# A transformer layer on one Trainium2 core: eight modulation units of the second norm's scale become whole rows summed by VectorE

## The chip, the cores and the metric

One core of a Trainium2 chip runs the whole layer in one launch. The metric is the device time of that launch in microseconds (us), as the median of several executions. The engines are TensorE (PE in the profile, its weight loads PEld), VectorE (DVE), ScalarE (ACT), GpSimd (POOL) and SyncE (SP), which issues nearly all DMAs here from one queue, in order. PE, ACT and DVE take their instructions in the order in which the program hands them over.

## The reference

One layer of a diffusion backbone on 128 context tokens and 512 latent tokens, width 1024, float32. Every norm is followed by a scale and a shift, and every branch by a gate; these six vectors are products of a conditioning vector with slices of `w_ada`, one vector for the context tokens and one for the latent ones:

```python
sh1, sc1, g1, sh2, sc2, g2 = jnp.split(ada, N_ADA, axis=-1)   # ada = silu(c) @ w_ada + b_ada, (.., 6 * 1024)
u = rms_norm(h, p["g_pre1"]) * (1 + sc1) + sh1
mo, k, v = mixer(u, p, rope_tabs, ctx_k, ctx_v)               # attention @ w_att_out, conv @ w_conv_out, gates, @ w_o
h = h + g1 * rms_norm(mo, p["g_post1"])
u = rms_norm(h, p["g_pre2"]) * (1 + sc2) + sh2
h = h + g2 * rms_norm(conv_ffn(u, p), p["g_post2"])
```

The change is about how `sc2`, the second norm's scale, is computed: 2 x 1024 numbers from 4 MB of weights. It is needed only when the second norm's output is turned and scaled, in the second half of the product with `w_o`.

## The kernel before

**Products in two parts.** Each float32 operand is cut into a rounded high part (ACT, `hi_of` L1253 or `split` L199) and a remainder (DVE, `lo_of` L1257 or `split` L200), and each product is made of three matmuls, high by high, high by low and low by high (`mm3`, L234 to L236, or `block`, L1266). So for each 512 KB of weights that SP loads into a `raw` slot (three of them), ACT and DVE each make one part (`whi`, `wlo`) before PE can use it.

**The stages that matter here**, in order of time:

- *Attention's output projection* (loop `for j in range(KT)`, 8 visits). Each visit cuts the next weights, makes some sums of the matrix that the next stage multiplies (`making`), and runs `plain_gemm`: 48 matmuls of 320 columns into two PSUM banks, `(2n + h) % 8` for visit n. Behind visits 0 to 4 stands `ada2_mm`: two *modulation units*, each 128 columns of `w_ada` (all 1024 rows, loaded by `ada2_load`, L283), multiplied by the conditioning vectors on PE in 32-column strips of its array (L289). Units 0 to 7 are the scale, units 8 and 9 the first quarter of the shift. DVE adds each pair's result to `acc` (L1485, L1487), and after visit 5 one small matmul and three DVE instructions (`ada2_fold`) put all ten into `mod`. Pair j is summed in bank `(2 * j + 4) % 8`, but pair 0 in bank 2.
- *The mixer's input products* (19 products, `mix`). Here the rest of the shift is already made from whole rows: SP loads 128 rows of `w_ada` at a time, DVE multiplies them by the conditioning value of its partition and sums them (`gate_add`, L341 for the first rows, L343 for the others), once for each of the two conditioning vectors, and at the end PE sums over the partitions with four matmuls against ones (`gate_sums`, L352).
- *w_conv_out* (8 visits of `plain_gemm`). Each visit on DVE: the next weights' low part, two multiplies by the gate (L1451), one addition (L1626), the low part of the result (L1280). Between them stand two `gate_add` of 1024 columns, which make the first gate, `g1`, from whole rows in the regions `GA0` and `GA1` (5 rows each).
- *The first half of w_o* (`for q in range(4)`, quarters of 30 matmuls of 512 columns: 5 token tiles, two blocks of 128 rows). Between the quarters PE sums the gate (`gate_sums`), DVE finishes it (`gate_rows`, L356 and L357), and SP writes it out and reads it back spread over all partitions. Loads and cuts for the second half run beside it (`half_load`, L2013; `half_cut`), and rooms are opened in `GA0` and `GA1` for the next product's right sides (`more_right`, which gives `ZBr`).
- *The second half of w_o*, in which each token tile is normed, scaled and shifted as it comes (`turn2`, L1735; `modulated`, L1746, which reads `mod`).

**What sets the order.** PE, ACT and DVE run in the order written out; SP's too up to the end of w_conv_out (`loads`), and from there a scheduler places SP's DMAs.

Of the kernel before, what the change touches and what calls it, by code (L numbers as in the profile page):

```python
# [20 lines left out]
KT = 8  # L21
# [90 lines left out]
def trunk_layer(ctx, tc, x_prompt, x_sample, cache_k, cache_v, c, c_ctx, w_ada, b_ada, g_pre1, g_post1, g_pre2,  # L112
# [30 lines left out]
    def nm(s):  # L143
        cnt[0] += 1
        return f"{s}_{cnt[0]}"
# [149 lines left out]
    def ada2_load(i, room=None):  # L295
        ada_raw[i] = raw_tile() if room is None else room
        ada_load(ada_raw[i], (4, 3)[i // KT] * D + (i % KT) * 128)

    def ada2_mm(us, p=None):

        p = (ps1() if p is None else p)[:, 0:128]
        for i in us:
            ada_mm(p, ada_raw[i], 2 * (i % 16), i == us[0], i == us[-1])
        return p
# [6 lines left out]
        else:  # L311
            V.tensor_tensor(out=a, in0=a, in1=p, op=ALU.add)

    def ada2_fold(acc, p=None):
        p = ps1() if p is None else p
        PE.matmul(p[:, 0:32], acc[:, 0:128], sel, start=True, stop=True)
        for which, nf in ((0, KT), (1, KT // 4)):
            src = p[:, 16 * which:16 * which + 2 * nf].rearrange("p (f r) -> p r f", r=2)
            b = F_B + (4, 3)[which] * KT
            V.tensor_tensor(out=mod[:, which, :, 0:nf], in0=src, in1=feat[:, b:b + nf].unsqueeze(1).broadcast_to((128, 2, nf)), op=ALU.add)  # L320
            if which == 0:
                V.tensor_tensor(out=mod[:, which], in0=mod[:, which], in1=feat[:, F_PRE2:F_PRE2 + KT].unsqueeze(1).broadcast_to((128, 2, KT)),
                                op=ALU.mult)


    def gate_load(raw, kind, k, c0=0):
        nc.sync.dma_start(raw, w_ada[k * 128:(k + 1) * 128, kind * D + c0:(kind + 1) * D])
# [974 lines left out]
    ada_rooms = {}  # L1302

    def ada2_fetch(i):
        h = i // 2 % 2
        if i % 2 == 0:
            ada_rooms[h] = rb.tile([128, 2, 1024], F32, tag=("r6b", "r5b")[h], name=nm("ada"))
        ada2_load(i, ada_rooms[h][:, i % 2])

    def quad(x, i):  # L1310
        return x[:, i * 4 * HT:(i + 1) * 4 * HT].rearrange("p (k c) -> p k c", k=4)
# [142 lines left out]


    acc = WB[:, 3200:3328]
    for i in range(4):
        ada2_fetch(i)
    for j in range(KT):
        unit = next_unit()  # L1460
        if j == 6:
            for n in range(3):
                mload(n)
        if j < 6:
            for f in making[2 * j:2 * j + 2]:
                f()
        elif j == 7:
            adds = msums(0)
            adds[0]()
            mhi(0, 0)  # L1470
            lo_of(("m", 0, 0))
            adds[1]()
            mhi(0, 1)
            adds[2]()
            mload(3)
        outs = plain_gemm(j, *unit.parts, AH, AL)
        for out, (b0, b1) in zip(outs, BLKS):
            if j < 2:
                times(MA[:, j, b0:b1], out, MA[:, KT - 2 + j, b0:b1])
            else:  # L1480
                S.activation(MA[:, j, b0:b1], out, AF.Copy)
        if j < 5:
            p = ada2_mm((2 * j, 2 * j + 1), bank((2 * j + 4) % 8 if j else 2))
            if j == 0:
                V.tensor_copy(acc, p)  # L1485
            else:
                V.tensor_tensor(out=acc, in0=acc, in1=p, op=ALU.add)  # L1487
            if j < 3:
                for i in (2 * j + 4, 2 * j + 5):
                    ada2_fetch(i)  # L1490
        elif j == 5:
            ada2_fold(acc, bank((2 * j + 4) % 8))


    BH = Halves(NTOK, F32R, "BH")
# [100 lines left out]

    GA0, GA1 = (region(ra, f"r{i}", [5, D], F32, f"GA{i}") for i in range(2))
    gaccs, gvec = [[GA0[:, i, :]] for i in range(2)], GA0[:, 4, :].rearrange("p (i c) -> p i c", i=2)
    graws = [GA1[:, k, :] for k in range(5)] + [GA0[:, k, :] for k in (2, 3)] + [GA1[:, 0, :]]


    loads = ctx.enter_context(ExitStack())
# [1 line left out]
    for j in range(KT):  # L1604
        if j + 1 < KT:
            vcut(j + 1)
        else:
            cut_upto(state["next"] + 1)
        if 0 < j < KT - 3:
            mload(2 * NP + j + 3)  # L1610
        elif j:
            fetch(state["next"] + min(j - 4, 2))
        if j == 0:
            gate_load(graws[0], 2, 0)
        if j < KT - 1:
            gate_load(graws[j + 1], 2, j + 1)
        if j == 5:
            gate_vectors(gvec, 2, g_post1)
        _, hi, lo = cut["v", j]
        outs = plain_gemm(j + 2, hi, lo, BH, BL)  # L1620
        sg = ROWS[j]
        for h, (out, (b0, b1)) in enumerate(zip(outs, BLKS)):
            times(sg[:, b0:b1], out, sg[:, b0:b1])
            if h == 0 and j:
                gate_add(gaccs, graws[j], j, 0)
        V.tensor_tensor(out=sg, in0=sg, in1=MA[:, j, :], op=ALU.add)  # L1626
        for row in range(0 if j == 0 else 1, 2):
            gate_add(gaccs, graws[j], j, row)
        mh, ml = MH[j // 4][:, j % 4, :], ML[j // 4][:, j % 4, :]
        S.activation(mh, sg, AF.Copy)  # L1630
        minus(ml, sg, mh.bitcast(F32))
# [12 lines left out]
        z = ra.tile([128, 2, 4, HALF], F32R, tag=f"r2{x}", name=f"ZB{i}")  # L1644
        TT[i] = (z[:, 0], z[:, 1])

    def more_right():
        for names, tag in ((("B11", "B21"), "r0"), (("B22", "T2"), "r1")):
            z = ra.tile([128, 4, 4, HALF], F32R, tag=tag, name=f"ZB{tag}")
            for a, i in enumerate(names):  # L1650
                TT[i] = (z[:, 2 * a], z[:, 2 * a + 1])

    QUAD = {f"{i + 1}{j + 1}": UFS[i][:, :, j * HALF:(j + 1) * HALF] for i in range(2) for j in range(2)}

# [365 lines left out]
    us = []  # L2020
    for q in range(4):
        us.append(next_unit())
        if q == 0:
            half_load(3)
            taps_load()
            for t in range(3):
                row_load(t)
            half_cut(3, lent("T3"))
        elif q == 1:
            half_load(0)  # L2030
            p = bank(6)
            gate_sums(p, gaccs)
            gate_rows(p, gvec, GA0[:, 3, 0:512], 0)
            half_cut(0)
        elif q == 2:
            half_load(1)
            plain_load(0, 0)
            plain_load(0, 1)
            for row in (1, 0):
                bload(WR[:, row, :], 0, row)  # L2040
            ffn_taps(bank(7))
        else:
            more_right()
            half_cut(1)
            half_load(2)
            for i, name in ((0, "T2"), (1, "T1")):
                hi_of((0, i), raws[0, i], lent(name))
                lo_of((0, i))
                plain_load(1, i)
        for t in range(NT):  # L2050
            if q == 0:
                PA[t] = bank(t)
            for k in (2 * q, 2 * q + 1):
                sl = slice(t * 128, (t + 1) * 128)
                mm3(PA[t], MH[k // 4][:, k % 4, sl], ML[k // 4][:, k % 4, sl], *us[q].at(k % 2), k == 0, k == KT - 1)


    KORDER = (0, 1, 2, 3, 6, 7, 4, 5)
# [307 lines left out]
```

## Time and profile before

| | us |
|---|---|
| three executions | 1092.72, 1093.31, 1094.11 (median 1093.31) |
| the profiled execution | 1094.45 |
| its span, first to last instruction | 1092.6 |
| DVE busy | 852.3 (78%) |
| ACT busy | 584.8 (54%) |
| DMA, mean over the span | 139 GB/s |

A row of a timeline reads: start, duration, engine, line of the program, operation, output and inputs, count, and in brackets how long the engine had been idle and what ended that. Matmuls overlap, so a row's duration is longer than its share of PE's time; starts of neighbours tell what a step costs. `SPq` is a DMA's issue on SP's queue. Names are the program's, without buffer numbers: `b` is a PSUM bank, `MHa` to `MLb` the two parts of w_o's left side, `GA` the two regions of row sums, `ada` the modulation units' weights, `s` the conditioning vectors.

### The profile page before, as it was taken

What the parts mean: (1) busy time and instruction counts of PE and PEld (TensorE: products, weight loads), DVE (VectorE), ACT (ScalarE), POOL (GpSimd) and SP (SyncE); (2) the same over time, 40 slices, a digit from 0 to 9 for tenths busy, and PEclk for the clock granted to TensorE, in tenths of its full rate; (3) what the DMA queues carried; (4) which work ended last, traced back from release to release, by engine and by line L of the source; (5) the groups of instructions that cost most, each with busy time, mean ns of one, the idle gap of its engine ahead of it and who ended that gap; (6) DMA issues with size and microseconds to landing.
All of it is one profiled execution on the core that took longest, in us unless ns stands there. A gap on an engine that the chain in (4) does not pass through costs nothing.

```text
span 1092.6 us, 20419 instructions
## 1 busy us (share of the span) xinstructions
PE 1073.0 (98%) x8155; PEld 998.1 (91%) x8155; DVE 852.3 (78%) x1313; ACT 584.8 (54%) x1050; POOL 130.9 (12%) x163
## 2 busy tenths in 40 slices
PE   8999999999999999999999999999999999999997
PEld 6788888899999999999999789999999999998886
DVE  5687888855578999987488368889999988989544
ACT  5468989952345454545423366655546555545442
POOL 1077666600000000000000020000000000000001
PEclk9999999999999999999999999999999999999999
DMA  9828999997144333332445634324434433335722
GB/s 322 246 69 159 168 163 189 180 179 204 58 119 126 95 92 93 91 95 86 152 135 184 195 128 136 103 91 125 137 106 131 137 102 110 120 102 197 271 78 97
DMA packets 245613, 152.18 MB, mean 139 GB/s; under 512 B 94602, under 2 KB 224134, under 8 KB 245518
## 3 DMA queue, kind: packets, MB, share of 16 engines
q1 hardware_dynamic: 245406, 150.84, 51.1%
q8 instruction: 64, 1.05, 0.4%
q14 instruction: 31, 0.25, 0.1%
q10 hardware_dynamic: 112, 0.04, 0.0%
HBM read 117.39 MB, written 11.44 MB: 118 GB/s over the span
## 4 chain that ended last, share of the span: by engine, by line
PE 87%; DVE 5%; DMA 4%; ACT 2%; issue 1%; POOL 0%; DVEq 0%; SPq 0%; ACTq 0%
PE b L1266 44%; PE b L234 10%; PE b L236 10%; PE b L235 10%; PE s L689 5%; PE s L1065 2%; PE s L1162 1%; DMA PT<-P 1%; DVE marks L1112 1%; DMA araw<-in_w_ada_dram 1%; PE s L234 1%; DMA raw<-in_w_in_dram 1%; DVE wlo L1257 1%; PE s L236 1%; PE s L235 1%
## 5 line engine op out<-in xcount | busy, mean ns | idle before, releaser
L1266 PE MATMUL b<-ZBr,whi 128*128 128x320 f32 x688 | 152.2, 309 | 0.0
L1266 PE MATMUL b<-MT,whi 128*128 128x320 f32 x608 | 134.3, 309 | 0.3 <-DVE WA L1277 0.3
L1266 PEld LDWEIGHTS b<-ZBr,whi 128*128 128x128 f32 x688 | 115.0, 188 | 0.1
L1266 PE MATMUL b<-ZBr,wlo 128*128 128x320 f32 x344 | 106.3, 309 | 0.0
L1266 PEld LDWEIGHTS b<-MT,whi 128*128 128x128 f32 x608 | 101.6, 188 | 0.6 <-issue 0.6
L1266 PE MATMUL b<-MT,wlo 128*128 128x320 f32 x304 | 94.1, 309 | 0.0
L1253 ACT ACTIVATE whi<-SUM 128x1024 fp32r<-128x1024 f32 x40 | 42.2, 1056 | 78.7 <-DVE SUM L1800 76.1
L1830 DVE SCALAR_TENSOR_TENSOR Y<-C,cffn,Y 128x642 f32<-128x642 f32 x88 | 77.6, 882 | 0.9
L1266 PE MATMUL b<-ZBT,whi 128*128 128x320 f32 x320 | 71.0, 309 | 0.0
L1266 PE MATMUL b<-UL,whi 128*128 128x320 f32 x228 | 70.8, 311 | 0.0
L1253 ACT ACTIVATE whi<-WB 128x1024 fp32r<-128x1024 f32 x38 | 40.1, 1055 | 56.4 <-DVE WB L1367 56.4
L1266 PE MATMUL b<-UH,wlo 128*128 128x320 f32 x228 | 70.1, 307 | 0.0
L1266 PE MATMUL b<-UH,whi 128*128 128x320 f32 x228 | 69.7, 306 | 0.0
L1257 DVE TENSOR_TENSOR wlo<-raw,whi 128x1024 fp32r<-128x1024 f32 (+1 forms) x51 | 50.4, 1018 | 22.6 <-ACT whi L1253 22.6
L200 DVE TENSOR_TENSOR wlo<-raw,whi 128x1024 fp32r<-128x1024 f32 (+1 forms) x31 | 34.2, 1102 | 40.3 <-ACT whi L199 39.8
L1266 PEld LDWEIGHTS b<-ZBr,wlo 128*128 128x128 f32 x344 | 64.6, 188 | 0.3 <-DVE wlo L1257 0.3
L1274 ACT ACTIVATE p<-b 128x320 f32<-128x320 f32 x78 | 34.2, 438 | 55.1 <-PE b L1266 53.4
L1266 PEld LDWEIGHTS b<-MT,wlo 128*128 128x128 f32 x304 | 57.0, 188 | 0.3 <-DVE wlo L1257 0.2
L1112 DVE TENSOR_REDUCE marks<-s 128x1 f32<-128x640 f32 x64 | 51.9, 815 | 6.5 <-PE s L1065 6.5
L1266 PEld LDWEIGHTS b<-ZBT,whi 128*128 128x128 f32 x320 | 54.2, 188 | 1.5
L1253 ACT ACTIVATE whi<-raw 128x1024 fp32r<-128x1024 f32 (+1 forms) x51 | 43.5, 892 | 18.4 <-PE b L236 10.0
L1257 DVE TENSOR_TENSOR wlo<-WB,whi 128x1024 fp32r<-128x1024 f32 x38 | 46.5, 1223 | 8.7 <-ACT whi L1253 8.6
(420 smaller groups left out, 3210.5 us busy)
## 6 DMA issues: line engine op xcount, KB each, us to landing
raw<-in_w_in_dram SPq DMA_DIRECT2D x48, 512.0 KB
RAW<-in_w_up_dram SPq DMA_DIRECT2D x40, 512.0 KB
raw<-in_w_down_dram SPq DMA_DIRECT2D x22, 512.0 KB
actd<-Y SPq DMA_DIRECT2D x18, 321.0 KB
ada<-in_w_ada_dram SPq DMA_DIRECT2D x10, 512.0 KB
XT<-in_w_ada_dram SPq DMA_DIRECT2D x9, 512.0 KB
raw<-in_w_att_out_dram SPq DMA_DIRECT2D x8, 512.0 KB
raw<-in_w_conv_out_dram SPq DMA_DIRECT2D x8, 512.0 KB
```

The source lines that it names most:

```text
L200: V.tensor_tensor(out=lo[:, :n], in0=raw, in1=hi[:, :n].bitcast(F32), op=ALU.subtract)
L234: PE.matmul(out, ah, bh, start=start, stop=False)
L235: PE.matmul(out, ah, bl, start=False, stop=False)
L236: PE.matmul(out, al, bh, start=False, stop=stop)
L689: PE.matmul(out, a, b, start=start and n == 0, stop=stop and n == 2, skip_group_check=True)
L1065: PE.matmul(o[h], q_of(hl, i, rows), kk[kx][rows, g, ks], start=m == 0, stop=m == 2, tile_position=(64 * h, 0), skip_group_check=True)
L1112: V.tensor_reduce(out=mk[:, h:h + 1], in_=s_of(), axis=AX.X, op=ALU.max, negate=True)
L1253: S.activation(to[0], raw, AF.Copy)
L1257: V.tensor_tensor(out=lo, in0=raw, in1=hi.bitcast(F32), op=ALU.subtract)
L1266: PE.matmul(out, p[:, ws], q[:, k, :], start=start and k == 0 and n == 0, stop=stop and k == 3 and n == 2, skip_group_check=True)
L1274: S.activation(t, pair[j][b], AF.Copy)
L1830: V.scalar_tensor_tensor(out=y, in0=crows(j)[i][:, d:d + NACT], scalar=cffn[:, 44 * d + o:44 * d + o + 1], in1=y, op0=ALU.mult, op1=ALU.add)
```

## The change

The eight scale units leave the attention projection; its one remaining pair (the two shift units) comes behind visit 1, in bank 6, and is folded behind visit 2 (`shift_fold`). The scale is made from whole rows instead, like the gate: `scale_load` loads 128 rows of `w_ada` (512 KB) into one of three rows of `GA1`, `scale_add` multiplies and adds 1024 columns on DVE, sixteen times in all (eight blocks of rows, two conditioning vectors), into `GA0`. Seven of them stand in w_conv_out's visits 1 to 7, three, two and four in w_o's quarters 0, 1 and 2. Within quarter 3, after its third token tile, PE sums over the partitions (`gate_sums` into bank 7), ACT copies the sums, and behind the quarter PE turns them into columns with four transposes and DVE adds the bias and multiplies by the gain (`scale_columns`, four instructions of 8 columns). The gate's own rows shrink from seven places to two, its finished rows go to `GA1`, and the room in `GA0` is opened only behind the transposes.

```diff
-    def ada2_fold(acc, p=None):
-        p = ps1() if p is None else p
+    def shift_fold(acc, p):
         PE.matmul(p[:, 0:32], acc[:, 0:128], sel, start=True, stop=True)
...
@@ attention's output projection
     acc = WB[:, 3200:3328]
-    for i in range(4):
-        ada2_fetch(i)
+    lent_ada = rb.tile([128, 2, 1024], F32, tag="r6b", name="ada")
+    for i in range(2):
+        ada2_load(KT + i, lent_ada[:, i])
     for j in range(KT):
...
-        if j < 5:
-            p = ada2_mm((2 * j, 2 * j + 1), bank((2 * j + 4) % 8 if j else 2))
-            if j == 0:
-                V.tensor_copy(acc, p)
-            else:
-                V.tensor_tensor(out=acc, in0=acc, in1=p, op=ALU.add)
-            if j < 3:
-                for i in (2 * j + 4, 2 * j + 5):
-                    ada2_fetch(i)
-        elif j == 5:
-            ada2_fold(acc, bank((2 * j + 4) % 8))
+        if j == 1:
+            V.tensor_copy(acc, ada2_mm((KT, KT + 1), bank((2 * j + 4) % 8)))
+        elif j == 2:
+            shift_fold(acc, bank((2 * j + 4) % 8))
...
-    graws = [GA1[:, k, :] for k in range(5)] + [GA0[:, k, :] for k in (2, 3)] + [GA1[:, 0, :]]
+    graws = [GA1[:, k % 2, :] for k in range(KT)]
+    saccs, sraws = [[GA0[:, 2 + i, :]] for i in range(2)], [GA1[:, 2 + k % 3, :] for k in range(KT)]
+
+    def scale_load(k):
+        gate_load(sraws[k], 4, k)
+
+    def scale_add(i):
+        gate_add(saccs, sraws[i // 2], i // 2, i % 2)
+
+    def scale_columns(p, rows):
+        for c in range(4):
+            PE.transpose(p[:, c * 128:(c + 1) * 128], rows[:, c * 128:(c + 1) * 128], ident)
+        to, b = mod[:, 0].rearrange("p r (h c) -> p r h c", h=2), F_B + 4 * KT
+        for f, op, x in ((b, ALU.add, p.rearrange("p (c h r x) -> p r h c x", h=2, r=2, x=32)[:, :, :, :, 0]), (F_PRE2, ALU.mult, to)):
+            for row in range(2):
+                V.tensor_tensor(out=to[:, row], in0=x[:, row], in1=feat[:, f:f + KT].rearrange("p (h c) -> p h c", h=2), op=op)
...
@@ w_conv_out, visit j
         if j < KT - 1:
             gate_load(graws[j + 1], 2, j + 1)
+        for k in ((0,), (1,), (), (2,), (), (3,), (4,), (5,))[j]:
+            scale_load(k)
...
         for row in range(0 if j == 0 else 1, 2):
             gate_add(gaccs, graws[j], j, row)
+        if j:
+            scale_add(j - 1)
...
@@ the first half of w_o
     for q in range(4):
         us.append(next_unit())
+        for i in ((7, 8, 9), (10, 11), (12, 13, 14, 15), ())[q]:
+            scale_add(i)
+            if i in (7, 9):
+                scale_load(i // 2 + 3)
...
             gate_sums(p, gaccs)
-            gate_rows(p, gvec, GA0[:, 3, 0:512], 0)
+            gate_rows(p, gvec, GA1[:, 0, 0:512], 0)
...
-            more_right()
+            more_right(("B22", "T2"), "r1")
...
                 mm3(PA[t], MH[k // 4][:, k % 4, sl], ML[k // 4][:, k % 4, sl], *us[q].at(k % 2), k == 0, k == KT - 1)
+            if q == 3 and t == 2:
+                p = bank(7)
+                gate_sums(p, saccs)
+                S.activation(GA0[:, 0, 0:512], p, AF.Copy)
+    scale_columns(bank(6), GA0[:, 0, 0:512])
+    more_right(("B11", "B21"), "r0")
```

How instructions stand on an engine before and after, at two places. First DVE in w_o's quarters 0 to 2, before, from the low part of quarter 1's weights (the first row) to the convolution taps' copy; `wlo` are weights' low parts, `ZBT` that of the second half's last block, `GA` the gate's two finishing instructions:

```order
L200 TENSOR_TENSOR wlo_7364<-raw_7232,whi_7363 128x1024
L1257 TENSOR_TENSOR ZBT_7359<-raw_7367,ZBT_7359 128x1024
L200 TENSOR_TENSOR wlo_7414<-raw_7361,whi_7413 128x1024
L356 TENSOR_TENSOR GA_6837<-b_537_7419,GA_6837 128x512
L357 SCALAR_TENSOR_TENSOR GA_6837<-GA_6837 128x512
L1257 TENSOR_TENSOR wlo_7431<-raw_7417,whi_7430 128x1024
L200 TENSOR_TENSOR wlo_7465<-raw_7411,whi_7464 128x1024
L1687 COPY cffn<-b_545_7476 128x132
```

And after, the same stretch:

```order
L200 TENSOR_TENSOR wlo_7291<-raw_7155,whi_7290 128x1024
L338 SCALAR_TENSOR_TENSOR GA_6751<-GA_6752,s_81,GA_6751 128x1024 x3
L1252 TENSOR_TENSOR ZBT_7286<-raw_7299,ZBT_7286 128x1024
L200 TENSOR_TENSOR wlo_7346<-raw_7288,whi_7345 128x1024
L338 SCALAR_TENSOR_TENSOR GA_6751<-GA_6752,s_81,GA_6751 128x1024 x2
L351 TENSOR_TENSOR GA_6752<-b_528_7353,GA_6751 128x512
L352 SCALAR_TENSOR_TENSOR GA_6752<-GA_6752,GA_6751 128x512
L1252 TENSOR_TENSOR wlo_7365<-raw_7351,whi_7364 128x1024
L200 TENSOR_TENSOR wlo_7399<-raw_7343,whi_7398 128x1024
L338 SCALAR_TENSOR_TENSOR GA_6751<-GA_6752,s_81,GA_6751 128x1024 x4
L1687 COPY cffn<-b_536_7414 128x132
```

Nine row sums have come in, in groups of three, two and four, each group between the low parts of two weights.

Second SP's queue in the same quarters, before: w_o's weights for quarter 2, then a block of the second half, the residual's rows (`WR`), the taps (`UFb`), the weights for quarter 3, two more blocks of the second half, and the gate's way out (`bct`):

```order
L216 DMA raw_7361<-in_w_o_dram 128x2x512
L2013 DMA raw_7367<-in_w_o_dram 128x2x512
L1682 DMA WR<-in_x_prompt_dram 128x1024
L1682 DMA WR<-in_x_sample_dram 128x1024 x2
L1679 DMA UFb<-in_conv_ffn_dram 88x128
L1679 DMA UFb<-in_conv_ffn_dram 44x128
L216 DMA raw_7411<-in_w_o_dram 128x2x512
L2013 DMA raw_7417<-in_w_o_dram 128x2x512
L2013 DMA raw_7468<-in_w_o_dram 128x2x512
L361 DMA bct<-GA_6837 1x512 x4
```

And after:

```order
L216 DMA raw_7288<-in_w_o_dram 128x2x512
L322 DMA GA_6752<-in_w_ada_dram 128x1024
L1682 DMA WR<-in_x_prompt_dram 128x1024
L1682 DMA WR<-in_x_sample_dram 128x1024
L2013 DMA raw_7299<-in_w_o_dram 128x2x512
L1682 DMA WR<-in_x_sample_dram 128x1024
L1679 DMA UFb<-in_conv_ffn_dram 88x128
L1679 DMA UFb<-in_conv_ffn_dram 44x128
L216 DMA raw_7343<-in_w_o_dram 128x2x512
L322 DMA GA_6752<-in_w_ada_dram 128x1024 x2
L2013 DMA raw_7351<-in_w_o_dram 128x2x512
L2013 DMA raw_7406<-in_w_o_dram 128x2x512
```

Three loads of scale rows (`GA` from `w_ada`) have come in, one ahead of the residual's rows and two ahead of the blocks `raw_7351` and `raw_7406`, which are the second half's blocks 0 and 1.

More of the change, by code (lines that the diff above doesn't have):

```diff
@@ L312, in ada2_keep @@
             V.tensor_tensor(out=a, in0=a, in1=p, op=ALU.add)
-    def ada2_fold(acc, p=None):
-        p = ps1() if p is None else p
+    def shift_fold(acc, p):
         PE.matmul(p[:, 0:32], acc[:, 0:128], sel, start=True, stop=True)
[L317 to L323, printed above, removed]
+        nf = KT // 4
+        V.tensor_tensor(out=mod[:, 1, :, 0:nf], in0=p[:, 16:16 + 2 * nf].rearrange("p (f r) -> p r f", r=2),
+                        in1=feat[:, F_B + 3 * KT:F_B + 3 * KT + nf].unsqueeze(1).broadcast_to((128, 2, nf)), op=ALU.add)
     def gate_load(raw, kind, k, c0=0):
@@ L1301, in trunk_layer @@
     TAG = {"T1": "r5a", "T2": "r5b", "T3": "r6a", "T4": "r6b"}
[L1302 to L1308, printed above, removed]
     def quad(x, i):
@@ L1645, in trunk_layer, with more_right @@
         TT[i] = (z[:, 0], z[:, 1])
[L1647 to L1651, printed above, removed]
+    def more_right(names, tag):
+        z = ra.tile([128, 4, 4, HALF], F32R, tag=tag, name=f"ZB{tag}")
+        for a, i in enumerate(names):
+            TT[i] = (z[:, 2 * a], z[:, 2 * a + 1])
     QUAD = {f"{i + 1}{j + 1}": UFS[i][:, :, j * HALF:(j + 1) * HALF] for i in range(2) for j in range(2)}
```

## The prediction

> **What bounds the kernel now.** I read the page first, then the table of stages (windows of engine time), then the waits of TensorE (PE) in these stages, then the timelines around the edits.
>
> ```profile
> span 1092.6 us, 20419 instructions
> PE 1073.0 (98%) x8155; PEld 998.1 (91%) x8155; DVE 852.3 (78%) x1313; ACT 584.8 (54%) x1050; POOL 130.9 (12%) x163
> PEclk9999999999999999999999999999999999999999
> PE 87%; DVE 5%; DMA 4%; ACT 2%; issue 1%; POOL 0%; DVEq 0%; SPq 0%; ACTq 0%
> ```
>
> PE is busy nearly all the span, at its full clock, and makes 87% of the chain that ends last. The stages of the edits (columns: window and its length, then busy us and instructions of PE, PEld, VectorE (DVE), ScalarE (ACT), POOL; granted clock, DMA share, GB/s), and PE's only wait in the first of them:
>
> ```profile
> 239.30:302.40 63.10, 62.58 (x546) 60.56 (x546) 33.99 (x37) 19.04 (x26) 0.00 (x0) 1.00 0.56 148
> 537.70:594.20 56.50, 56.50 (x386) 56.50 (x385) 43.59 (x52) 14.47 (x18) 0.00 (x0) 1.00 0.53 170
> 594.20:624.40 30.20, 30.20 (x135) 23.36 (x134) 14.40 (x16) 9.22 (x10) 0.00 (x0) 1.00 0.67 217
> PE b L234 <- DVE WB L1485: 0.5, 1, 0.5
> ```
>
> The rows are attention's output projection, w_conv_out, and the first half of w_o. All three are PE's: what leaves PE's queue is gained whole, what enters it is paid whole, and what DVE gets is free until an operand comes late.
>
> **What leaves PE.** Visits 0, 2, 3 and 4 of attention's output projection lose their pair of modulation units; visit 1 keeps one. PE's timeline at visits 0 and 1:
>
> ```profile
> 246.37 0.30 PE L236 MATMUL b<-AHb,wlo 128*128 128x320 f32 x1
> 246.61 1.08 PE L289 MATMUL b<-ada,s 128*32 128x128 f32 x32
> 248.19 0.39 PE L234 MATMUL b<-AHa,whi 128*128 128x320 f32 x1 [0.51 <-DVE WB L1485]
> 248.42 0.31 PE L235 MATMUL b<-AL,whi 128*128 128x320 f32 x1
> ...
> 255.17 0.31 PE L236 MATMUL b<-AHb,wlo 128*128 128x320 f32 x1
> 255.41 1.08 PE L289 MATMUL b<-ada,s 128*32 128x128 f32 x32
> 256.42 0.42 PE L234 MATMUL b<-AHa,whi 128*128 128x320 f32 x1
> 256.67 0.31 PE L235 MATMUL b<-AL,whi 128*128 128x320 f32 x1
> ```
>
> From a visit's second matmul (248.42) to its 48th (255.17) are 46 steps, 0.147 us each. Without the pair the next visit's second matmul would start two steps after 255.17, at 255.46; it starts at 256.67. A pair costs 1.20 us of the path, more than its busy 1.08, since the matmul behind it also starts slowly. After visit 0 it is 248.42 - (246.37 + 0.29) = 1.76: pair 0 writes bank 2, which is visit 1's first output bank, so PE waits 0.51 for DVE to copy the sum out (L1485). The change puts its one pair in bank 6 at visit 1, which visit 3 uses first, so that wait leaves too. The fold (one small matmul) only moves from visit 5 to visit 2. Gain: 1.76 + 3 x 1.20 = 5.36 us. If the wait stayed it would be 4.85. A visit becomes 48 x 0.147 = 7.05 us instead of 8.26. By the stage's row DVE and ACT then have 34 and 19 us of work in some 58, and the changed program drops eight 512 KB loads there, so no other engine binds.
>
> **What enters PE.** In w_o's last quarter come four column sums of 512 and, behind the quarters, four transposes. Both have twins in the trace:
>
> ```profile
> 600.74 0.40 PE L235 MATMUL b<-wlo,MHa 128*128 128x512 f32 x1
> 600.98 0.40 PE L236 MATMUL b<-whi,MLa 128*128 128x512 f32 x1
> 601.30 1.07 PE L352 MATMUL b<-GA,ones 128*32 128x512 f32 x8
> 602.30 0.50 PE L234 MATMUL b<-whi,MHa 128*128 128x512 f32 x1
> 602.63 0.40 PE L235 MATMUL b<-wlo,MHa 128*128 128x512 f32 x1
> ...
> 636.10 0.39 PE L236 MATMUL b<-whi,MLa 128*128 128x512 f32 x1
> 636.33 0.60 PE L1735 MATMUL b<-ident,TX 128*128 128x128 f32 x4
> 636.68 0.48 PE L234 MATMUL b<-whi,MHa 128*128 128x512 f32 x1
> 637.00 0.39 PE L235 MATMUL b<-wlo,MHa 128*128 128x512 f32 x1
> ```
>
> A step is 0.23 to 0.24 (600.74 to 600.98). By the same reckoning the sums cost 602.63 - (600.98 + 0.46) = 1.19 and four transposes 637.00 - (636.10 + 0.46) = 0.44: together 1.63 us, if nothing waits.
>
> **What DVE gets in w_conv_out.** One visit there:
>
> ```profile
> 566.20 0.49 DVE L1451 TENSOR_TENSOR WA<-b,WA 128x320 f32<-128x320 f32 x1 [1.05 <-PE b L236]
> 566.72 0.82 DVE L1626 TENSOR_TENSOR WA<-WA,MA 128x640 f32<-128x640 f32 x1
> 567.47 1.28 DVE L343 SCALAR_TENSOR_TENSOR GA<-GA,s,GA 128x1024 f32<-128x1024 f32 x1
> 568.66 0.82 DVE L1280 TENSOR_TENSOR MLa<-WA,MHa 128x640 fp32r<-128x640 f32 x1
> 569.40 1.22 DVE L1257 TENSOR_TENSOR wlo<-raw,whi 128x1024 fp32r<-128x1024 f32 x1
> 570.53 0.48 DVE L1451 TENSOR_TENSOR WB<-b,WB 128x320 f32<-128x320 f32 x1
> 570.93 1.27 DVE L343 SCALAR_TENSOR_TENSOR GA<-GA,s,GA 128x1024 f32<-128x1024 f32 x1
> 573.25 0.49 DVE L1451 TENSOR_TENSOR WB<-b,WB 128x320 f32<-128x320 f32 x1 [1.04 <-PE b L236]
> ```
>
> DVE starts its next instruction 1.19 us after a row sum, so it is free at 572.12 and PE's next half comes at 573.25: 1.13 us of room in 7.05. Visits 1 to 7 get one sum each, 0.06 too much, so by 573.25 + 3 x 7.05 = 594.4, the end of visit 7, DVE is at most 0.4 us late (the first two sums only multiply and should cost less). The weight part that PE needs next (L1257) then ends at 569.40 + 1.19 + 1.22 = 571.8, plus up to 0.4, and PE needs it at about 573.4: hidden, with over 1 us left. The gate's loads now wait for a free row (two rows instead of seven): the load for visit j+1 starts when visit j-1's last sum ends, say at 568.7 for the sum at 570.93 + 7.05 = 578.0, 9 us ahead.
>
> **What DVE gets in w_o.** Nine sums go into its gaps:
>
> ```profile
> 602.43 0.69 DVE L356 TENSOR_TENSOR GA<-b,GA 128x512 f32<-128x512 f32 x1 [1.34 <-PE b L352]
> 608.91 1.23 DVE L1257 TENSOR_TENSOR wlo<-raw,whi 128x1024 fp32r<-128x1024 f32 x1 [5.06 <-ACT whi L1253]
> 599.99 1.50 SPq L2013 DMA_DIRECT2D raw<-in_w_o_dram  x2
> 607.82 1.06 ACT L1253 ACTIVATE whi<-raw 128x1024 fp32r<-128x1024 f32 x1 [8.44 <-DMA raw<-in_w_o_dram]
> ```
>
> On the clock of before, a quarter of w_o on PE is 30 steps, 7.0 us: with the gate's sums behind the first and the taps' transposes (taken as 0.44) behind the second, quarters 1, 2 and 3 start at 602.4, 609.9 and 616.8. I lay DVE's new order end to end: from 594.8 the multiply, add, gate sum, scale sum and difference take 4.4 us; then (each weight part 1.14, each sum 1.19) one part, three sums, two parts, two sums, the gate's two rows (0.73 each), two parts: the parts for quarters 1, 2 and 3 end near 600.4, 606.3 and 612.4, all ahead of PE. The last four sums end near 617.2 and the taps' copy near 617.8. PE reaches the new sums 18 matmuls into quarter 3, at 616.8 + 4.2 = 621.0. So on paper 3 us are left.
>
> What eats them is a load. The scale's last two rows wait in SP's queue for DVE's sums, and behind them stands w_o's second-half load 0, whose slot now comes free at 605.2 instead of 599.99. Its ACT part started 7.8 us after its issue (599.99, 607.82); with 7.8 again it starts at 613.0, ACT does quarter 3's part behind it, DVE's four sums end near 621.2, the taps' copy (whose bank the sums take) near 621.8, and PE waits 0.8. If the load is as quick as the queue allows (5 us), PE waits nothing. I take 0.2, nearer to nothing, since the residual's row loads that the quoted load stood behind are long over at 605; bounds 0 and 1.5.
>
> The Trainium skill, DMA: Bandwidth & Descriptors, section "Anatomy of one DMA", fits one transfer as 2.0 us plus its bytes over 436 GB/s, an estimate of 3.2 us for 512 KB; by it the load would be there at 608.4 and the wait nil, while the trace's 7.8 us behind other loads says that the queue, not the one transfer, decides.
>
> Behind the waits: behind the new sums on PE stand two token tiles of quarter 3 and all of w_o's second half; behind the copy of the sums on ACT the last weight part and the squares; behind the four small `mod` instructions on DVE the same part's difference, due six of eight steps (4.2 us) into the second half. ACT's copy is ready some 2 us before PE has done the two tiles, so the transposes do not wait.
>
> **Sum.** -5.36 + 1.63 + 0.2 = -3.5 us. Against the profiled execution (1094.45 us, its span plus 1.85) that is 1090.9; the median of the three runs lies 1.14 lower, so 1093.31 - 3.5 = 1089.8 us.
>
> **Rivals.**
> (1) Quarter 3 comes late: load 0 starts its ACT part at 614 to 618 rather than 611 to 613, and PE gives back 2 to 5 us at quarter 3 or at the new sums. For it: the sums spend DVE's idle time here (5.06 in one piece). Against it: that load lags 0.67 of DMA share, not a full one. With 2.5 given back, 1092.3.
> (2) The projection gives less: some visit stays near 7.5 us because weights, ScalarE or banks bind once the pairs are gone, or the 0.51 stays. Against it: the stage's row. Four visits at 7.5 give back 4 x 0.45 = 1.8 us: 1091.6; the wait alone, 0.51: 1090.3.
> (3) Slower: the last scale row lands late. The scale's loads 6 and 7 take turns behind VectorE's sums, and the four last sums, the first second-half weight room (which lies in the scale's rows and waits for them), ACT's copy and the transposes hang on it in one chain. It decides from 3.7 us of standstill, when nothing is left of the gain; at 5.9 the four sums end at 626.9 and the time is 1093.31 - 5.36 + 1.63 + 5.9 = 1095.5. That takes a load of over 14 us; the quoted one took 7.8.
> The Trainium skill, TensorE: Matmul & The Clock Gate, Part 1, says that an idle window of about 3.4 us halves PE's clock, which would add by estimate up to 1.7 us to such a standstill; no run here shows it, the granted clock being full in all 40 slices.
>
> **Numbers.** Forecast 0.70; rival 1 0.14; rival 2 0.10; rival 3 0.06. What a measurement can tell from no change is 0.2%, 2.2 us. Faster: the forecast, 0.06 of rival 2 and 0.02 of rival 1, 0.78. Same: 0.04 and 0.12, 0.16. Slower 0.06. The forecast's own bounds are a gain of 3.7 (no wait) to 1.7 (4.85, 1.63, 1.5), with 0.7 for the spread of runs (1092.72 to 1094.11): 1088.7 to 1092.0, which also takes in rival 2.
>
> **What would show it.** Right: visits of 7.05 us with one pair left, and w_conv_out starting 5.3 us earlier; DVE without idle time in w_conv_out's visits 3 to 7 and PE still without a wait there; the new sums 1.2 and the transposes 0.45 on PE; the second half of w_o some 3.6 us earlier than before. Wrong: a gap on PE before quarter 3 or the sums, with a load or DVE's GA as releaser, or a projection that keeps 8 us visits.

## The result, and the profile after

The changed kernel takes 1089.82 us, the median of six executions (1089.23 to 1091.58), beside 1094.32 for the kernel before (1092.72 to 1095.29); the medians differ by 4.5 us. The ratio of the means, which the tables below give, is 0.9963 [0.995, 0.9976], some 4.0 us less. A second series gave 1090.63 beside 1094.15, ratio 0.9969 [0.9958, 0.998], some 3.4 us. The forecast was 3.5 us less, 1089.8 us.

The profiled execution took 1091.58 us. Its span, PE's row of busy time, and the clock's row of the slices:

```profile
span 1089.8 us, 20200 instructions
PE 1071.4 (98%) x8039; PEld 997.3 (92%) x8039; DVE 869.0 (80%) x1327; ACT 585.3 (54%) x1051; POOL 131.2 (12%) x163
PEclk9999999999999999999999999999999999999999
```

PE stays the bound at 98%. The same stages as before, in the view of windows (window and length, busy us and instructions of PE, PEld, DVE, ACT, POOL, then granted clock, DMA share, GB/s), from each stage's first matmul to the next stage's:

```profile
240.40:298.30 57.90, 57.90 (x418) 57.51 (x419) 32.49 (x31) 18.95 (x26) 0.00 (x0) 1.00 0.32 91
533.60:590.06 56.46, 56.46 (x387) 56.46 (x385) 48.88 (x58) 14.47 (x18) 0.00 (x0) 1.00 0.69 218
590.06:621.14 31.08, 31.08 (x144) 23.20 (x143) 26.51 (x27) 9.26 (x10) 0.00 (x0) 1.00 0.74 240
```

Attention's output projection shrank to 57.9 us, w_conv_out kept its length with 5 us more work on DVE, and w_o's first half grew to 31.1 with 26.5 us on DVE instead of 14.4. The row of before reaches to 624.40, three matmuls into the second half; from first matmul to first matmul (594.21 to 623.76) the first half took 29.55 there, so it grew by 1.53, and the slow start behind the transposes adds another 0.1. PE's timeline at the pair that is left, at the new column sums and at the new transposes:

```profile
254.41 0.31 PE L236 MATMUL b<-AHb,wlo 128*128 128x320 f32 x1
254.65 1.08 PE L289 MATMUL b<-ada,s 128*32 128x128 f32 x32
255.66 0.42 PE L234 MATMUL b<-AHa,whi 128*128 128x320 f32 x1
255.91 0.31 PE L235 MATMUL b<-AL,whi 128*128 128x320 f32 x1
...
616.58 0.39 PE L236 MATMUL b<-whi,MLb 128*128 128x512 f32 x1
616.90 1.06 PE L347 MATMUL b<-GA,ones 128*32 128x512 f32 x8
617.89 0.50 PE L234 MATMUL b<-whi,MHb 128*128 128x512 f32 x1
618.23 0.40 PE L235 MATMUL b<-wlo,MHb 128*128 128x512 f32 x1
...
620.56 0.39 PE L236 MATMUL b<-whi,MLb 128*128 128x512 f32 x1
620.79 0.60 PE L1592 MATMUL b<-ident,GA 128*128 128x128 f32 x4
621.14 0.48 PE L234 MATMUL b<-whi,MHa 128*128 128x512 f32 x1
621.46 0.40 PE L235 MATMUL b<-wlo,MHa 128*128 128x512 f32 x1
```

No row has a wait. By the prediction's own reckoning the pair costs 255.91 - (254.41 + 0.29) = 1.21, the sums 618.23 - (616.58 + 0.46) = 1.19 and the transposes 621.46 - (620.56 + 0.46) = 0.44 us. The other engines in w_o, in their timelines:

```profile
589.32 1.27 DVE L338 SCALAR_TENSOR_TENSOR GA<-GA,s,GA 128x1024 f32<-128x1024 f32 x1
590.51 0.48 DVE L1439 TENSOR_TENSOR WB<-b,WB 128x320 f32<-128x320 f32 x1
...
597.34 2.73 SPq L322 DMA_DIRECT2D GA<-in_w_ada_dram  x2
600.87 1.51 SPq L2013 DMA_DIRECT2D raw<-in_w_o_dram  x2
...
608.11 1.06 ACT L1248 ACTIVATE whi<-raw 128x1024 fp32r<-128x1024 f32 x1 [9.57 <-DMA raw<-in_w_o_dram]
609.21 1.23 DVE L1252 TENSOR_TENSOR wlo<-raw,whi 128x1024 fp32r<-128x1024 f32 x1 [3.51 <-ACT whi L1248]
611.48 4.86 DVE L338 SCALAR_TENSOR_TENSOR GA<-GA,s,GA 128x1024 f32<-128x1024 f32 x4
616.27 0.28 DVE L1687 COPY cffn<-b 128x132 f32<-128x132 f32 x1
618.29 0.58 ACT L2063 ACTIVATE GA<-b 128x512 f32<-128x512 f32 x1
```

Second-half block 0 is issued at 600.87 and used at 608.11, 7.2 us later. DVE idles 3.51 us for it, then does quarter 3's weight part and the four last sums, and frees the sums' bank with the copy of the taps at 616.27 + 0.28 = 616.55. PE's next step is due at 616.58 + 0.23 = 616.81. So 0.26 us of room is left where the prediction's paper had 3.

### The profile page after: what moved, and what is told of

Same layout as the page of the kernel before. It is cut to its first block, busy times and chain, and to the rows that moved or that the text cites. A ratio compares the mean times of both kernels' runs of the same rounds, so it can differ in the third digit from the quotient of the medians.

```text
span 1089.8 us, 20200 instructions
## 1 busy us (share of the span) xinstructions
PE 1071.4 (98%) x8039; PEld 997.3 (92%) x8039; DVE 869.0 (80%) x1327; ACT 585.3 (54%) x1051; POOL 131.2 (12%) x163
## 4 chain that ended last, share of the span: by engine, by line
PE 86%; DVE 6%; DMA 4%; ACT 2%; issue 1%; POOL 0%; SPq 0%; DVEq 0%; ACTq 0%
PE b L1261 43%; PE b L234 10%; PE b L236 10%; PE b L235 10%; PE s L684 5%; PE s L1060 2%; PE s L1157 1%; DMA PT<-P 1%; DVE wlo L1252 1%; DVE marks L1107 1%; DMA raw<-in_w_in_dram 1%; PE s L234 1%; DMA araw<-in_w_ada_dram 1%; PE s L236 1%; PE s L235 1%
```

## The experiments

Executions of one kernel differ by 1 to 6 us, so effects under 1 us are read from stages of the profiled execution. The ratio is that of the means, each kernel against executions of the kernel before in its own series. In this table the projection runs from its first matmul to the next stage's; "w_o" from its first matmul to the first transposes of the second norm's output, in its second half; "rest" from the projection's first matmul to the last matmul of the program, which leaves out what ran before the edits.

| kernel | median, us | ratio to before [95%] | projection | w_o | rest |
|---|---|---|---|---|---|
| before | 1094.3 | | 63.29 | 42.12 | 847.2 |
| changed | 1089.8 | 0.9963 [0.995, 0.9976] | 57.92 | 43.74 | 843.4 |
| e1 projection alone | 1088.5 | 0.9951 [0.9935, 0.9967] | 57.92 | 42.05 | 842.1 |
| e2 no new matmuls | 1089.5 | 0.9959 [0.9943, 0.9975] | 57.92 | 42.93 | 842.6 |
| e3 no row sums | 1090.1 | 0.9969 [0.9958, 0.998] | 57.93 | 43.71 | 843.4 |
| e4 bank of pair 0 | 1093.9 | 0.9995 [0.9984, 1.0006] | 62.76 | 42.12 | 846.4 |
| e5 five sums last | 1091.0 | 0.9972 [0.9962, 0.9982] | 57.93 | 44.01 | 843.7 |
| e6 two sums last | 1090.6 | 0.9967 [0.9956, 0.9979] | 57.92 | 43.71 | 843.5 |
| e7 no matmuls, two last | 1089.8 | 0.996 [0.9948, 0.9972] | 57.93 | 42.84 | 842.6 |
| e8 late row | 1097.8 | 1.0036 [1.0023, 1.0049] | 57.94 | 49.65 | 848.9 |
| e9 own rooms, no matmuls | 1090.6 | 0.996 [0.9946, 0.9975] | 57.93 | 42.06 | 841.6 |
| e10 own rooms | 1090.6 | 0.9967 [0.9955, 0.998] | 57.92 | 43.71 | 843.6 |
| e11 six sums last | 1091.6 | 0.9975 [0.9964, 0.9987] | 57.91 | 44.97 | 844.5 |
| e12 changed, again | 1090.6 | 0.9969 [0.9958, 0.998] | 57.93 | 44.00 | 843.8 |

### The three parts, one at a time

**e1**, the projection's edit alone:

```diff
 def scale_load(k):
-    gate_load(sraws[k], 4, k)
+    pass
 def scale_add(i):
-    gate_add(saccs, sraws[i // 2], i // 2, i % 2)
+    pass
...
-                gate_sums(p, saccs)
-                S.activation(GA0[:, 0, 0:512], p, AF.Copy)
-    scale_columns(bank(6), GA0[:, 0, 0:512])
+    V.memset(mod[:, 0], 0.5)
```

> The change without the scale's new way: the 16 sums of whole rows, their eight loads, the four column sums and the four transposes are left out, and the scale is set to a constant. Only the edit of attention's output projection stays. Theory (the projection gives 5.36 us, what enters w_o costs 1.63, the sums on VectorE cost nothing): 5.4 us below the kernel before, 1.6 below the changed kernel, and a projection of 57.9 us in the profile. Rival (the projection's gain is partly given back behind it, and w_o's part is cheaper than its 1.63): 3.5 to 4.5 us below the kernel before.

Measured: ratio 0.9951, some 5.4 us below the kernel before; projection 57.92, which is 5.37 less than before; w_o 42.05, 1.69 less than the changed kernel. The theory holds, and the projection's gain reaches the end.

**e2**, e1's last four lines only, so that the sums on DVE stay:

```diff
-                gate_sums(p, saccs)
-                S.activation(GA0[:, 0, 0:512], p, AF.Copy)
-    scale_columns(bank(6), GA0[:, 0, 0:512])
+    V.memset(mod[:, 0], 0.5)
```

> The changed kernel without the four column sums, ScalarE's copy of them and the four transposes; the scale is a constant, while the 16 sums and their loads stay and nobody reads them. Theory: the whole cost in w_o is TensorE's, so 5.4 us below the kernel before, as with the projection alone, and w_o's first half 29.8 us long. Rival (the sums on VectorE and their loads cost part of it, by weight parts that come late): 0.5 to 1.5 us slower than the projection alone, with a wait of TensorE at a quarter of w_o.

Measured: w_o 42.93, 0.88 more than e1. By the whole times the two can't be told apart (0.9959 and 0.9951, the intervals overlap), but PE's and DVE's timelines show a wait:

```profile
621.84 1.23 DVE L1252 TENSOR_TENSOR wlo<-raw,whi 128x1024 fp32r<-128x1024 f32 x1 [3.91 <-ACT whi L1248]
622.14 0.40 PE L234 MATMUL b<-whi,MHb 128*128 128x512 f32 x1
623.12 0.50 PE L235 MATMUL b<-wlo,MHb 128*128 128x512 f32 x1 [0.58 <-DVE wlo L1252]
```

This is the weight part of w_o's second-half block 2. So the rival is right here, though at the second half and not at a quarter: the work on DVE does cost, once PE comes earlier.

**e3**, the reverse: the matmuls stay, the sums go.

```diff
+    G.memset(GA0[:, 2:4, :], 0.01)
 def scale_load(k):
-    gate_load(sraws[k], 4, k)
+    pass
 def scale_add(i):
-    gate_add(saccs, sraws[i // 2], i // 2, i % 2)
+    pass
```

> The changed kernel without the 16 sums of whole rows and their eight loads; the rows that they would leave are set once to a constant by GpSimd, and the four column sums, the copy and the transposes stay. Theory: VectorE's sums lie wholly under TensorE's work, so the time of the changed kernel (3.7 us below the kernel before), and w_o's first half 31.4 us long. Rival (the sums cost): faster than the changed kernel by 0.5 to 1.5 us.

Measured: w_o 43.71 against 43.74, and a ratio equal to the changed kernel's second series. Beside PE's new 1.63 us the 16 sums and their loads cost nothing in this profile of the changed kernel, and 0.29 in the other (44.00, e12 below). With e1 and e2: matmuls alone cost 1.66, sums alone 0.88, both together 1.69. The two do not add up, because PE's new work is also the cover that hides block 2.

**e4**, the kernel before with one number changed:

```diff
-            p = ada2_mm((2 * j, 2 * j + 1), bank((2 * j + 4) % 8 if j else 2))
+            p = ada2_mm((2 * j, 2 * j + 1), bank((2 * j + 4) % 8))
```

> The kernel before with one number changed: the first pair of units in attention's output projection writes bank 4 instead of bank 2. Theory (the pair's 0.51 us of waiting is the bank that visit 1 writes first): no wait of TensorE there, the pair costs 1.2 like the others, 0.5 us below the kernel before. Rival (the wait has another cause, the weights or VectorE): the wait stays, no change.

PE's timeline there:

```profile
246.56 0.31 PE L236 MATMUL b<-AHb,wlo 128*128 128x320 f32 x1
246.80 1.08 PE L289 MATMUL b<-ada,s 128*32 128x128 f32 x32
247.81 0.42 PE L234 MATMUL b<-AHa,whi 128*128 128x320 f32 x1
248.06 0.31 PE L235 MATMUL b<-AL,whi 128*128 128x320 f32 x1
```

The wait of 0.51 is gone, pair 0 costs 248.06 - (246.56 + 0.29) = 1.21 like the others, and the projection is 0.53 shorter. The ratio of the whole times (0.9995 [0.9984, 1.0006]) does not show it.

### How near the edge w_o runs

**e5, e6 and e11** move sums between w_o's quarters:

```diff
-        for i in ((7, 8, 9), (10, 11), (12, 13, 14, 15), ())[q]:
+        for i in ((7, 8, 9), (10,), (11, 12, 13, 14, 15), ())[q]:      # e5
+        for i in ((7, 8, 9), (10, 11, 12, 13), (14, 15), ())[q]:       # e6
+        for i in ((7, 8, 9), (), (10, 11, 12, 13, 14, 15), ())[q]:     # e11
```

> The changed kernel with sum 11 moved from w_o's quarter 1 to quarter 2, so that five sums of 1.19 us stand ahead of the taps' copy instead of four. Theory (in the profiled run VectorE's copy of the taps ends at 616.6, TensorE reaches the new sums at 616.8: the room is about 0.2 us): TensorE waits about 1 us at the new sums for VectorE's copy of the taps, 1.0 us slower than the changed kernel, 2.8 below the kernel before. Rival (the prediction's paper: 3 us of room): no wait, the changed kernel's time.

> The changed kernel with sums 12 and 13 moved from quarter 2 to quarter 1, into the 3.5 us that VectorE idles there before w_o's second-half block 0 arrives. Theory (TensorE waits for nothing in w_o now): the changed kernel's time, 3.7 us below the kernel before, with VectorE's copy of the taps done some 2.4 us before TensorE reaches the sums. Rival (a hidden wait at the new sums is part of the 1.6 us that w_o's first half grew): up to 0.4 us faster than the changed kernel, and a first half under 31.2 us.

> The changed kernel with sums 10 and 11 moved from quarter 1 to quarter 2: six sums ahead of the taps' copy. With five, TensorE waited 0.2 us in the profiled run. Theory: each more sum is 1.19 us of wait, so 1.4 us here, give or take the 0.6 us by which block 0's arrival differs between runs; 0.8 to 2.0 us slower than the changed kernel, and, the standstill being short, a granted clock of 1.00 behind it (it was 0.63 behind one of 4.35 us). Rival (the room is larger than the one profile showed): 0 to 0.3 us slower. Rival on the clock: any standstill lowers it.

Measured: e5 has a wait of 0.2 us at the new sums and w_o is 0.27 longer than the changed kernel's, not 1.0; in its profiled execution block 0 landed 6.6 us after its issue and not 7.2, which gave back 0.6 of the 1.19. The length alone would not tell it, since two profiles of the changed kernel differ by 0.26 (e12); the wait's row does. e6 has no wait and the changed kernel's length. The sums in e5, then in e11:

```profile
615.26 1.06 PE L347 MATMUL b<-GA,ones 128*32 128x512 f32 x8 [0.23 <-DVE cffn L1687]
```

```profile
615.88 1.07 PE L347 MATMUL b<-GA,ones 128*32 128x512 f32 x8 [1.21 <-DVE cffn L1687]
```

In e11 the wait is 1.21, w_o 1.23 longer than the changed kernel's, the median 1.0 above the second series'. Block 0 landed 6.4 us after its issue there, so 2 x 1.19 less the room of 0.26 and the 0.8 given back is 1.3. So the room is 0 to 0.3 us, not 3, with 0.6 of play by how soon block 0 lands. The sums behind that wait took 1.07, as without it.

**e8** makes the slower rival's chain: the scale's last row waits for the place of the row before it.

```diff
-    saccs, sraws = [[GA0[:, 2 + i, :]] for i in range(2)], [GA1[:, 2 + k % 3, :] for k in range(KT)]
+    saccs, sraws = [[GA0[:, 2 + i, :]] for i in range(2)], [GA1[:, 2 + min(k, 6) % 3, :] for k in range(KT)]
...
-            if i in (7, 9):
-                scale_load(i // 2 + 3)
+            if i in (7, 13):
+                scale_load(6 + i // 13)
```

> The changed kernel with the scale's last row loaded into the place of the row before it: its load then waits for sum 13, in quarter 2. This is the slower rival's chain, made on purpose. Theory (the chain of last row, sums, taps' copy, column sums lies on TensorE's path as soon as 0.2 us of room are used): the load leaves at 613.9 on the changed kernel's clock, lands in 3 to 5 us, TensorE stands still 3 to 5 us at the column sums and the time is 3 to 5 us above the changed kernel, within 1.3 us of the kernel before. Rival (3 us of room on paper): 0 to 2 us above the changed kernel. If the granted clock falls behind a standstill of over 3.4 us, up to 1.7 us more; if not, the clock's row shows 1.00 there.

The timelines of SP, DVE and PE, and two windows of the same execution:

```profile
608.12 0.33 SPq L322 DMA_DIRECT2D GA<-in_w_ada_dram  x1
616.01 2.48 DVE L338 SCALAR_TENSOR_TENSOR GA<-GA,s,GA 128x1024 f32<-128x1024 f32 x2 [7.92 <-DMA GA<-in_w_ada_dram]
618.75 1.42 PE L347 MATMUL b<-GA,ones 128*32 128x512 f32 x8 [4.35 <-DVE cffn L1687]
621.55 0.63 PE L234 MATMUL b<-whi,MHb 128*128 128x512 f32 x1
621.98 0.63 PE L235 MATMUL b<-wlo,MHb 128*128 128x512 f32 x1
...
624.18 0.60 PE L1592 MATMUL b<-ident,GA 128*128 128x128 f32 x4
```

```profile
618.75:621.00 2.25, 2.25 (x10) 0.96 (x11) 2.25 (x3) 2.25 (x3) 0.00 (x0) 0.63 0.00 0
621.00:624.20 3.20, 3.20 (x12) 2.46 (x12) 1.33 (x2) 0.01 (x1) 0.00 (x0) 0.73 0.73 226
```

The row landed 7.9 us after its issue, behind w_up's and the gate's loads, and PE stood still 4.35 us. That lies in the theory's 3 to 5, but by two errors that cancel: the load left 20.6 us after w_o's start and not 23.8, since block 0 landed in 3.9 us here, and it took 7.9 us and not 3 to 5. Then PE's clock was low, 0.50 in the window from 620 to 622: the steps took 0.43 us instead of 0.23, and from the sums to the transposes 5.43 us passed instead of 3.89. Standstill and clock, 4.35 + 1.54, make the 5.91 us by which w_o grew. The median is 7 to 8 us above the changed kernel's, beyond the 3 to 5 expected; the profiled execution was the quickest of the six (1094.98). The other five had a mean granted clock of 0.993 to 0.994 over their span, it had 0.996; by estimate 0.002 to 0.003 of 1093 us is 2 to 3 us of the 2 to 5 by which they were longer. They have no profile, so where they lost it stays open.

### What makes the second half late

**e7** is e2 with e6's groups, to free block 2's slot sooner.

> The kernel without the four column sums, the copy and the four transposes (the scale a constant, its 16 sums of rows read by nobody), and with sums 12 and 13 in quarter 1. In the same kernel with four sums last TensorE waited 0.6 us in w_o's second half for the weight part of block 2, whose load waits for a slot that VectorE frees behind the four sums. Theory (the four sums delay that load): the wait is gone, and from w_o's start to the first transposes behind it 42.1 us as with the projection alone, instead of 42.9; 5.4 us below the kernel before. Rival (the load of block 2 is late by itself, or other loads delay it): the wait of 0.6 stays.

Measured: the wait stays (0.5), w_o 42.84. The theory fell. The timelines of SP and ACT:

```profile
610.45 1.53 SPq L1758 DMA_DIRECT2D raw<-in_w_up_dram  x2
615.55 0.38 SPq L2013 DMA_DIRECT2D raw<-in_w_o_dram  x1
622.52 1.06 ACT L1248 ACTIVATE whi<-raw 128x1024 fp32r<-128x1024 f32 x1 [2.96 <-DMA raw<-in_w_o_dram]
```

Counted from w_o's start, block 2's load (615.55) left 2.0 us sooner than in e2, at 25.3 instead of 27.2, and was used no sooner, at 32.2 instead of 32.3: it took 7.0 us from issue to use instead of 5.1. w_up's loads and the gate's stand ahead of it in the queue, some 2 us ahead here and over 4 in e2, which makes them the likely cause; e9 bears it out. They leave when DVE has done block 0's part, and that is late because block 0 is.

**e9** keeps e2's cut and moves the scale's last two rows into places that come free earlier, so that their loads leave 6 to 10 us sooner; **e10** is the whole changed kernel with the same places.

```diff
-    saccs, sraws = [[GA0[:, 2 + i, :]] for i in range(2)], [GA1[:, 2 + k % 3, :] for k in range(KT)]
+    saccs, sraws = [[GA0[:, 2 + i, :]] for i in range(2)], [GA1[:, 2 + k % 3 if k < 6 else k - 6, :] for k in range(KT)]
...
-        for k in ((0,), (1,), (), (2,), (), (3,), (4,), (5,))[j]:
+        for k in ((0,), (1,), (), (2,), (), (3,), (4,), (5, 6))[j]:
...
+    scale_load(7)
 loads.close()
...
-            if i in (7, 9):
-                scale_load(i // 2 + 3)
...
-            gate_rows(p, gvec, GA1[:, 0, 0:512], 0)
+            gate_rows(p, gvec, GA1[:, 3, 0:512], 0)
```

> Again without the four column sums, the copy and the four transposes (the scale a constant, its 16 sums of rows read by nobody), but the scale's last two rows are loaded into the two places that the gate's last rows leave, in visits 7 and behind it, so that they no longer wait for the scale's own sums; the gate's finished rows go to another place. Theory now (second-half block 0 stands in SyncE's queue behind the scale's last loads; its weight part frees the slot of w_up's first load, and block 2's load comes last in that chain): block 0 is issued about 5.8 us after w_o's start instead of 10.8, w_up's first load follows at 15 to 16 us instead of 19.8, the wait of 0.5 to 0.6 us for block 2's weight part is gone and w_o to the next transposes takes 42.1 us; 5.4 us below the kernel before. Rival (the bytes of the sums' rows in the same stretch delay block 2 wherever they stand): the wait stays, 42.8.

The timelines of SP and ACT in e9:

```profile
601.74 1.51 SPq L2014 DMA_DIRECT2D raw<-in_w_o_dram  x2
605.72 1.06 ACT L1248 ACTIVATE whi<-raw 128x1024 fp32r<-128x1024 f32 x1 [4.65 <-DMA raw<-in_w_o_dram]
608.07 1.53 SPq L1759 DMA_DIRECT2D raw<-in_w_up_dram  x2
```

The wait is gone and w_o takes 42.06, as in e1. But one step of the theory was wrong: block 0 left no sooner, 10.8 us after w_o's start as in the changed kernel, since its slot comes free with a weight part that stands behind DVE's sums. It landed sooner, 4.0 us after its issue instead of 7.2 in the changed kernel and 6.6 in e2; w_up's loads then followed at 17.2 us instead of 20.4 and 19.8. In the changed kernel the scale's last row was issued 1.1 us ahead of block 0; in e9 nothing was issued in the 4.7 us before it. That it need not be a scale row shows in e1, which loads none. There w_o's own weights are issued 1.1 us ahead (at 593.76), and block 0 takes 7.0 us all the same, in SP's and ACT's timelines:

```profile
594.89 1.50 SPq L2013 DMA_DIRECT2D raw<-in_w_o_dram  x2
601.87 1.06 ACT L1248 ACTIVATE whi<-raw 128x1024 fp32r<-128x1024 f32 x1 [7.58 <-DMA raw<-in_w_o_dram]
```

So e2's wait takes both: block 0 issued at 10.8 us after w_o's start and not at 5.8 as in e1, and a load just ahead of it. e1 lacks the first, e9 the second, and neither waits.

e9's whole times show less than the 5.4 us expected, 4.4 by the ratio. Three of its five executions had a mean granted clock of 0.995 and took 1090.6 to 1090.8 us, the other two 0.998 and 1088.4 to 1088.6.

> The changed kernel, whole, with the same other places for the scale's last two rows. Theory (only TensorE's 1.63 us binds in w_o): the changed kernel's time, w_o to the next transposes 43.7 us, but VectorE's copy of the taps ends 3 to 3.6 us before TensorE reaches the column sums instead of 0.2 to 0.3. Rival (the places make other loads late): a wait at w_o's quarters, 0.5 to 1.5 us slower.

Measured: w_o 43.71 without a wait, and the copy of the taps done 3.3 us before PE reaches the sums. The time is the changed kernel's, 1090.63 both in one series. No experiment points to a version that would be quicker than the change by more than can be measured; e10 has its time with over ten times the room.

**e12** is the changed kernel again, beside e9 to e11.

> The changed kernel as it is, beside the two runs above on the same chip. Theory: 3.7 us below the kernel before, within 0.6 us of the kernel with the other places; projection 57.9 us, w_o to the next transposes 43.7 us in its profile; and block 0's load takes 6.6 to 7.3 us from issue to use, as in the other profiles.

Measured: projection 57.93, and block 0 took 7.1 us from issue to use, as expected; w_o 44.00, which is 0.26 more than in the first profile and than expected. DVE's and PE's timelines show where:

```profile
621.77 1.23 DVE L1252 TENSOR_TENSOR wlo<-raw,whi 128x1024 fp32r<-128x1024 f32 x1 [2.67 <-ACT whi L1248]
622.66 0.40 PE L234 MATMUL b<-whi,MHb 128*128 128x512 f32 x1
623.05 0.50 PE L235 MATMUL b<-wlo,MHb 128*128 128x512 f32 x1
623.39 0.39 PE L236 MATMUL b<-whi,MLb 128*128 128x512 f32 x1
```

PE's first two rows lie 0.39 apart instead of 0.23, and the second starts slowly: the weight part of block 2 again, late by a fraction of a step. Block 2's load took 5.7 us from issue to use here and 5.2 in the first profile.

## Why the prediction was right

**The projection** was forecast at 5.36 us and measured at 5.37 (63.29 to 57.92). Both parts stand: pairs of 1.20 (1.21 for the one that is left), and the wait of 0.51, which e4 shows to have been the bank. Rival 2 is out.

**The matmuls in w_o**, 1.19 and 0.44, were measured to the digit, since both had twins in the trace. w_o grew by 1.62 in one profile and 1.88 in the other. The term of 0.2 for a wait came out as 0 and 0.26. So the stages sum up to -3.75 us in one profile and -3.48 in the other, beside the -3.5 of the forecast. Counted from the projection's first matmul, w_conv_out starts 5.13 us earlier and the second half of w_o 3.61 earlier, where 5.3 and 3.6 were named as signs. That the median of 1089.82 meets the 1089.8 so closely is luck: the three executions that the forecast started from have a median of 1093.31, the six beside the result one of 1094.32.

**The place of that wait was wrong.** The prediction put it at the taps' copy, ahead of the new sums; there nothing waited. It lies at block 2's weight part in the second half, which the prediction named as standing behind the sums' chain and gave no price.

**The room of 3 us on paper was mis-sized.** The prediction's own warning, that block 0's load eats it, is what happened: it left at 600.87 (605.2 on the clock of before, less the 4.15 us by which w_o now starts earlier, is 601.05) and took 7.2 us, near the upper of the two bounds, and the room was 0.26. The reason given for a quicker load, that the residual's rows would be long over, did not hold: the load's time goes with what is issued just ahead of it, and a 512 KB load was, 1.1 us before, in both kernels. With 7.2 us the prediction's formula would have given 0.2 of wait. What held is that the slot sets when the load leaves; the load issued 1.1 us ahead of it, here the scale's last row, goes with its late landing (e9 against the changed kernel, and e1).

**DVE's work counts as free only in this order.** In w_conv_out it went as forecast: full from visit 3, the last visit's multiply at 590.51 some 0.3 us late, no wait of PE. In w_o e3 shows the sums free and e2 shows them to cost 0.88 if PE's new work is not there to cover them.

**Rival 1**, quarter 3 late, did not occur. **Rival 3** did not occur, but e8 shows its chain at work: 4.35 us of standstill plus the clock made w_o 5.9 us longer. That 5.9 is also the figure used for the rival is chance, since there it was standstill alone, from a load of over 14 us; in e8 the load took 7.9. The prediction held that the clock was full in all 40 slices; the row of slices can't show that, as a 9 there stands for 90% or more, and the window of 90 to 93 us in the trace of before has 0.54. The Trainium skill, TensorE: Matmul & The Clock Gate, Part 1, has the clock halve after an idle window of about 3.4 us and stay so for about as long; by the prediction's estimate that adds up to 1.7 us. e8 agrees: a granted clock of 0.50, and 1.54 us lost, in some 4 us behind the standstill. The Trainium skill's fit for one transfer (DMA: Bandwidth & Descriptors, "Anatomy of one DMA"), by estimate 3.2 us for 512 KB, is given there for transfers that GpSimd issues, while SP issues these. Block 0 took 4.0 us in e9, with nothing just ahead of it, and 7.2 in the changed kernel.

**A slip in the range.** By its own terms, a gain of 3.7 to 1.7 from 1093.31 with 0.7 on either side, the range is 1088.9 to 1092.3 and not 1088.7 to 1092.0. Both medians lie in either.

## What to carry to other kernels

Price a moved operation by the pitch of its twin in the trace, from the matmul before it to the second behind it, and the sum can come out within a tenth of a microsecond where the engine is the bound, as here. What is free beside it holds only as long as the next late load allows: ask which slot frees the load, what stands just ahead of it in the queue, and how much room is left, and take the long time seen for a load and not the short one. Two costs that hide each other do not add up, so take each away alone before naming either.

## What the runs showed of the hardware

- A standstill of 4.35 us on TensorE was followed by a granted clock of 0.63 and 0.73 in the next 2.25 and 3.20 us (e8); behind one of 1.21 us the same sums took 1.07, at full speed (e11).
- The 512 KB load of block 0 took 3.9 to 4.2 us from issue to use where nothing had been issued in the 3.5 us before it (e8, e9, e10), and 6.4 to 7.8 where another 512 KB load had been issued 1.1 us before (the eleven other profiles).
- The changed kernel's two profiled executions differ by the clock granted early in them. The views of windows show 60 to 90 us, ahead of every edit:

```profile
60.00:90.00 30.00, 26.77 (x239) 24.73 (x237) 24.92 (x58) 19.00 (x45) 24.62 (x25) 0.94 0.14 37
```

```profile
60.00:90.00 30.00, 26.34 (x251) 24.29 (x251) 25.89 (x62) 20.53 (x49) 26.16 (x27) 1.00 0.21 52
```

The first (1091.58 us) reaches the projection at 240.38, the second (1089.08 us) at 237.48: more than the whole difference between them arises ahead of the change. The low clock stands in two stretches of the first, 69 to 75 us (0.81 and 0.62 by halves) and 90 to 96 (0.72 and 0.71), where the second has 1.00. Ahead of the later one PE waits 1.1 and then 1.2 us in both executions, so the same waits went with a lower clock in one and not in the other.
